# Split projection weights kept in DRAM and read back, and q/k/v products issued in steps of 24 matmuls

## The chip, the cores and the metric

One core of a Trainium2 chip. A core has five engines that run their own instruction streams and wait for each other by semaphores: PE (TensorE, the matrix multiplier), DVE (VectorE), ACT (ScalarE), POOL (GpSimd) and SP (SyncE, which here only issues DMA transfers). Work is held in SBUF (128 partitions) and matmuls add up in PSUM, in banks of 128 x 512 float32. The metric is the device time of one execution in microseconds (us), as the median of several runs.

## The reference

One inference step of a one-layer streaming encoder on 1024 prompt tokens and 64 sample tokens, width 1024, all in float32:

```python
h = _rms_norm(x, norm1_g)
parts = split(h @ w_in)                 # q,k,v (3 x 512), z 512, b 4, a 4, u 256, vm 256, sq 256, sk 128, sv 128
o_a = gated delta rule (q, k, v, a, b)  # 4 heads of 128: state S 128 x 128, blocks of 64 tokens, in sequence
o_b = spatial gating MLP (u, vm)        # 4 heads of 64
o_c = sliding-window attention (sq, sk, sv)
x = x + concatenate([o_a, o_b, o_c]) @ w_out
h = _rms_norm(x, norm2_g)
x = x + (silu(h @ w_gate) * (h @ w_up)) @ w_down      # D_FF 2816
```

The gated delta rule is a recurrence over blocks of 64 tokens: the state S that a block leaves is what the next block starts from, so its steps stand in a chain. The outputs are the new x and the caches and states.

## The kernel before, in words

**Numbers in two parts.** PE multiplies float32 rounded to a shorter format (`fp32r`). To keep float32's accuracy each operand is split into a high part (`h`, a rounded copy) and a low part (`l`, what the rounding left), and a big product is three matmuls: h by xh, h by xl, l by xh.

**Weights.** The class `Weights` holds a list of 84 pieces of [128, up to 1056], in the order of use. `load` issues the raw piece from DRAM by SP (512 KB, line 120) into one of three `wr` buffers; `split` makes the high part on ACT (`hw<-wr`, line 86) and the low part on DVE (`lw<-wr,hw`, line 92), each in two halves of 512 columns, into one of three slots (`hw`/`lw`); `pump`, `run` and `flush` set when a split is put between other work. The in-projection runs over three segments of tokens (384, 384 and 256+64). Each uses the same 24 pieces, in the order: two for the gates and the keys and values of the attention ("g0"), two for its queries ("sq"), twelve for q, k and v of the delta rule ("p"), two "u", two "vm", four "z"; so w_in is loaded and split three times. The out-projection works on w_out in halves of columns: pieces of half 0, of half 1, and once more of half 0 (`wo_plan[0]`, `[1]`, `[2]`, four pieces each, with a fourth slot, `he`/`le`).

**Order of the work.** The whole program is written in the order in which the engines run it. The in-projection's generator (`in_proj`, the main one) and up to a dozen helpers (`aux`) are advanced in turn by `drive`. The helpers are: the convolution of a q, k or v piece (`conv`), the preparation of a block (`prep`), the recurrence (`chain`), attention (`swa`, `q_norm`, `k_norm`) and the gating MLP (`u_evac`, `gmlp`). A round of `drive` is: every helper, in order of its priority, issues its next step as long as the steps of the round need no more than 6 PSUM banks (`ax`); then the main one issues its big matmuls; then each helper of the round goes on to its next halt. So PE's stream alternates between a block of big matmuls (`mm<-xh,hw` and so on) and a set of small ones (mostly `ax<-...`). `fm_group` writes the 24 big matmuls of a piece of q/k/v, u or z in two halves of 12, with a halt in the middle, where a set of small ones is put.

After the in-projection `drain` runs what is left of the helpers. `out_proj` then does 12 jobs of 24 matmuls (128 x 512), and two functions for the last segment's tokens follow: the one on half 1, then the one on half 0 (here "the last piece of the out-projection", which uses `wo_plan[2]`), while ACT and DVE make the operands (`w`, `x`) of the FFN. The FFN uses a scheme of seven products in the manner of Strassen from about 630 us to the end (`x,w` matmuls of line 1462); the change doesn't touch it.

## Time and profile before

| what | value |
|---|---|
| median of 3 runs | 1357.01 us (1356.85 to 1358.77) |
| the profiled execution | 1357.18 us, its span 1355.2 us |
| PE busy | 1316.4 us (97% of the span), 9922 matmuls |
| DVE, ACT, POOL busy | 986.2, 683.4, 183.4 us |
| mean granted clock of TensorE | 0.996 |
| DMA moved | 189.00 MB, of which HBM read 135.72 MB, written 51.61 MB |
| chain that ended last | PE 83%, issue 6%, DVE 5%, ACT 2%, DMA 2% |

How to read it: the in-projection and the recurrence run from the start to about 498 us, the out-projection to about 630 us, the FFN from there on. In rows of groups, `mm<-xh,hw 128*128 128x384` is a matmul into a tile `mm` from the tiles `xh` and `hw`, with the shape of its weights and of its moving operand; `x4` is a count. A row of the timeline has the start, the duration, the engine and line, the instruction, and in brackets the idle time before it and what ended that. Matmuls overlap, so what one adds to PE's time is the distance from its start to the next start, not its duration.

### The profile page before, as it was taken

The page shows a single profiled execution, that of the slowest core. Times are in us where ns is not written, and L with a number is a line of the kernel's source. Part 1 is how long each engine was busy: PE and PEld are TensorE (multiplying, and loading weights), DVE is VectorE, ACT ScalarE, POOL GpSimd, SP SyncE. Part 2 cuts the span into 40 slices and gives each one's busy share as a digit, 9 for nine tenths or more (in the row PEclk, how much of TensorE's full clock was granted, in tenths as well). Part 3 has the DMA queues.
Part 4 walks back from the last instruction along what each step waited for, and adds up shares of the span by engine and source line. Part 5 has one row for each costly group of instructions (what it writes and reads, how often), then busy time and mean ns, then how long its engine had stood idle before and what let it go on. Part 6 is the DMA issues. An engine that isn't in the chain of part 4 may idle for free.

```text
span 1355.2 us, 26537 instructions
## 1 busy us (share of the span) xinstructions
PE 1316.4 (97%) x9922; PEld 1170.9 (86%) x9922; DVE 986.2 (73%) x2286; ACT 683.4 (50%) x1725; POOL 183.4 (14%) x250
## 2 busy tenths in 40 slices
PE   6999999999999999998999999999999988999997
PEld 6988888888878887787999999999999976777784
DVE  6887877867788785588866777667776687767764
ACT  7677376674667653556555554455544532222202
POOL 3100130101121210100000000000000343232104
PEclk9999999999999999998999999999999999999999
DMA  8422342223233161322434544355443499666645
GB/s 259 122 79 64 82 116 78 79 64 80 70 93 94 49 214 51 121 78 86 126 120 152 176 136 124 111 156 175 132 124 112 159 320 335 223 225 238 215 142 198
DMA packets 205011, 189.00 MB, mean 139 GB/s; under 512 B 13931, under 2 KB 174160, under 8 KB 204882
## 3 DMA queue, kind: packets, MB, share of 16 engines
q1 hardware_dynamic: 196690, 174.71, 41.8%
q10 hardware_dynamic: 6704, 8.36, 1.7%
q0 software_dynamic: 1488, 4.23, 0.9%
q8 instruction: 78, 1.28, 0.4%
q14 instruction: 51, 0.42, 0.1%
HBM read 135.72 MB, written 51.61 MB: 138 GB/s over the span
## 4 chain that ended last, share of the span: by engine, by line
PE 83%; issue 6%; DVE 5%; ACT 2%; DMA 2%; POOL 1%; POOLq 0%; SPq 0%; ACTq 0%; DVEq 0%
PE ax L1462 29%; PE mm L95 26%; PE ax L95 11%; PE ax L1775 8%; PE mm L1462 5%; DVE x L92 2%; PE mm L1775 1%; PE ax L503 1%; PE ax L275 1%; DVE lw L92 1%; POOL x L1789 1%; PE ax L838 1%; DMA hd<-w 1%; DMA xs<-in_x_prompt_dram 0%; DVE tr L89 0%
## 5 line engine op out<-in xcount | busy, mean ns | idle before, releaser
L1462 PE MATMUL ax<-x,w 128*128 128x256 f32 (+1 forms) x2552 | 358.6, 287 | 0.0
L1462 PEld LDWEIGHTS ax<-x,w 128*128 128x128 f32 x2552 | 334.2, 190 | 0.3 <-ACT x L86 0.2
L92 DVE TENSOR_TENSOR w<-w,w 128x512 fp32r<-128x512 f32 (+1 forms) x242 | 164.6, 689 | 85.0 <-PE ax L1462 54.1
L95 PE MATMUL mm<-xh,hw 128*128 128x384 f32 (+1 forms) x432 | 151.3, 350 | 0.0
L95 PE MATMUL mm<-xl,hw 128*128 128x384 f32 (+1 forms) x432 | 143.5, 332 | 0.0
L95 PE MATMUL mm<-xh,lw 128*128 128x384 f32 (+1 forms) x432 | 143.1, 331 | 0.0
L92 DVE TENSOR_TENSOR x<-ax,x 128x512 f32<-128x512 f32 (+1 forms) x144 | 98.4, 687 | 58.2 <-PE ax L1775 47.7
L1775 PE MATMUL ax<-x,w 128*128 128x512 f32 x480 | 130.9, 397 | 9.6 <-DVE x L92 9.6
L86 ACT ACTIVATE hw<-wr 128x512 fp32r<-128x512 f32 (+2 forms) x168 | 99.7, 619 | 65.6 <-PE mm L95 55.0
L92 DVE TENSOR_TENSOR lw<-wr,hw 128x512 fp32r<-128x512 f32 (+2 forms) x168 | 110.8, 674 | 25.0 <-ACT hw L86 24.3
L1775 PEld LDWEIGHTS ax<-x,w 128*128 128x128 f32 x480 | 90.3, 190 | 33.1 <-DVE x L92 13.6
L1462 PE MATMUL ax<-xr,w 128*128 128x288 f32 x616 | 116.0, 296 | 1.2 <-DVE s L92 1.2
L86 ACT ACTIVATE w<-w 128x512 fp32r<-128x512 f32 x154 | 94.8, 624 | 31.4 <-PE mm L1462 14.4
L1462 PEld LDWEIGHTS ax<-xr,w 128*128 128x128 f32 x616 | 94.9, 188 | 1.5 <-DVE s L92 1.5
L95 PEld LDWEIGHTS mm<-xh,hw 128*128 128x128 f32 x432 | 81.1, 188 | 10.1 <-issue 7.3
L86 ACT ACTIVATE s<-ax 128x256 f32<-128x256 f32 (+1 forms) x132 | 51.9, 394 | 74.1 <-PE ax L1462 73.7
L95 PEld LDWEIGHTS mm<-xl,hw 128*128 128x128 f32 x432 | 81.4, 189 | 1.3 <-issue 0.7
L95 PEld LDWEIGHTS mm<-xh,lw 128*128 128x128 f32 x432 | 81.1, 188 | 1.2 <-issue 0.3
L1775 PE MATMUL ax<-f,w 128*128 128x512 f32 x220 | 72.5, 399 | 2.8 <-ACT w L86 1.6
L1678 POOL TENSOR_TENSOR w<-x 128x512 f32<-128x512 f32 x6 | 8.9, 1490 | 488.7 <-PE ax L1462 442.1
L1462 PE MATMUL mm<-x,w 128*128 128x256 f32 (+1 forms) x528 | 70.6, 289 | 0.0
L89 DVE SCALAR_TENSOR_TENSOR tr<-tr,cw 128x384 f32<-128x384 f32 (+1 forms) x108 | 64.1, 594 | 7.2 <-ACT tr L86 6.2
(360 smaller groups left out, 2551.0 us busy)
## 6 DMA issues: line engine op xcount, KB each, us to landing
wr<-in_w_in_dram SPq DMA_DIRECT2D x72, 512.0 KB, 3.9
hd<-e SPq DMA_DIRECT2D x140, 256.0 KB, 2.3
w<-hd SPq DMA_DIRECT2D x140, 256.0 KB, 4.6
w<-in_ffn_w_gate_dram SPq DMA_DIRECT2D x44, 256.0 KB, 3.5
w<-in_ffn_w_up_dram SPq DMA_DIRECT2D x44, 256.0 KB, 3.4
x<-in_ffn_w_down_dram SPq DMA_DIRECT2D x12, 512.0 KB, 3.7
wr<-in_w_out_dram SPq DMA_DIRECT2D x9, 512.0 KB, 4.4
y<-in_x_prompt_dram SPq DMA_DIRECT2D x8, 512.0 KB, 7.7
```

The source lines that it names most:

```text
L86: return A.activation(out=out, in_=in_, func=AF.Copy, scale=scale)
L89: return V.scalar_tensor_tensor(out=out, in0=in0, scalar=s, in1=in1, op0=op0, op1=op1)
L92: return V.tensor_tensor(out=out, in0=in0, in1=in1, op=op)
L95: return T.matmul(out, lhsT, rhs, start=start, stop=stop)
L275: T.transpose(b[k // 4][:, (k % 4) * r:(k % 4) * r + r], x[:r, k * 128:k * 128 + 128], ident[:r, :r])
L503: T.transpose(b[u // 4][:, (u % 4) * 128:(u % 4) * 128 + 128], src(u).rearrange("p h i -> p (h i)"), ident)
L838: T.transpose(PTp[0:r0 + cnt, j, kv, :], P[:, kv, 128 * j:128 * j + r0 + cnt], ident)
L1462: T.matmul(ps[:, :NB[c]], a[:, k, :], b[:, k, :], start=first and i == 0, stop=i == 11, skip_group_check=not first)
L1678: eng.tensor_tensor(out=block(t), in0=a, in1=b, op=ALU.subtract)
L1775: T.matmul(ps, l, r, start=fresh and m == 0, stop=m == 3 * len(kps) - 1, skip_group_check=not fresh)
L1789: G.tensor_tensor(out=yf[t][:, c], in0=block(slot), in1=yf[t][:, c], op=ALU.add)
```

## The change

**Kept splits.** A piece that is used again is split once. `keep(i, *later)` gives piece i a DRAM tile `wk` [2, 128, 1056] and notes the later uses in `again`. When piece i is split, SP also writes its high and its low part to that tile (two transfers of 512 KB). A later use issues no raw load and no split: SP reads both parts straight into the slot (two transfers of 512 KB), at the place in the program where the split stood. Kept are: segment 0's p, u, vm and z (20 pieces, read back in segments 1 and 2), segment 1's g0 and sq (4 pieces, read back in segment 2) and `wo_plan[0]` (4 pieces, read back as `wo_plan[2]`). So 36 pieces are split instead of 84, 28 are written, and 48 times a pair is read.

**Whole steps.** For q/k/v of segments 0 and 1 `fm_group` writes all 24 matmuls in one step (`whole`), so a piece has one set of small matmuls behind it and not two.

**Order of the helpers.** `conv` and `u_evac` go first in a round (priority -1) and count no banks; then come those that stand in the middle of a unit of their work (`held`), then the rest. `prep` turns v before the decay factors, and `q_norm` squares in two halves in `tr` buffers.

```diff
+        def keep(self, i, *later):
+            self.kept[i] = tc.dram_tile([2, 128, 1056], F32, name="wk%d" % i)
+            for j in later:
+                self.again[j] = self.kept[i]
         def load(self):
             i = self.nd
+            if i in self.again:
+                self.nd += 1
+                return
...
             h = sb(p, [128, 1056], "h" + t, F32R)
             l = sb(p, [128, 1056], "l" + t, F32R)
-            m = b if i < 2 else n // 2
-            for c in range(0, n, m):
-                acopy(h[:, c:c + m], r[:, c:c + m])
-                tt(l[:, c:c + m], r[:, c:c + m], h[:, c:c + m].bitcast(F32), ALU.subtract)
+            if i in self.again:
+                for j, x in enumerate((h, l)):
+                    SP.dma_start(out=x[:, :n].bitcast(F32), in_=self.again[i][j, :, :n])
+            else:
+                r = self.raw.pop(i)
+                m = b if i < 2 else n // 2
+                for c in range(0, n, m):
+                    acopy(h[:, c:c + m], r[:, c:c + m])
+                    tt(l[:, c:c + m], r[:, c:c + m], h[:, c:c + m].bitcast(F32), ALU.subtract)
+                if i in self.kept:
+                    for j, x in enumerate((h, l)):
+                        SP.dma_start(out=self.kept[i][j, :, :n], in_=x[:, :n].bitcast(F32))
...
+    parts = [pieces(d) for d in plan]
+    for i, j in zip(parts[1][0], parts[2][0]):
+        W.keep(i, j)
+    for i, j, k in zip(*[q[1] for q in parts]):
+        W.keep(i, j, k)
+    for i, j in zip(wo_plan[0], wo_plan[2]):
+        W.keep(i, j)
...
-    def fm_group(xh, xl, n, piece, evac):
+    def fm_group(xh, xl, n, piece, evac, whole=False):
...
-            if kk:
+            if kk and not whole:
                 vstep()
                 W.pump()
                 yield
...
-            if kk == 0:
+            if kk == 0 and not whole:
                 yield
...
-                yield from fm_group(xh, xl, n, piece, lambda ps, a=(s, g, kind, hp): spawn(1, 1, conv(*a, ps)))
+                yield from fm_group(xh, xl, n, piece, lambda ps, a=(s, g, kind, hp): spawn(-1, 0, conv(*a, ps)), s < 2)
...
-            for a in list(aux):
-                if a not in aux:
-                    continue
+            for a in sorted(aux, key=lambda a: 0 if a[0] < 0 else 1 if a in held else 2):
...
                     try:
-                        next(a[2])
+                        if next(a[2]) != "unit":
+                            held.append(a)
```

How the order moves, at the three places of which the prediction speaks.

PE, q/k/v of segment 1. Before, a piece (here `hw_2716`) is cut by a set of small matmuls after 12 big ones. `x4` behind a small matmul counts matmuls in the row:

```order
L95 MATMUL ax<-S_166,KQ 64x128 x4
L95 MATMUL mm<-xh,hw_2716 128x384
L95 MATMUL mm<-xl,hw_2716 128x384
L95 MATMUL mm<-xh,lw_2717 128x384
...
L95 MATMUL mm<-xh,lw_2717 128x384
L95 MATMUL ax<-w,Z 64x128 x2
L95 MATMUL mm<-xh,hw_2716 128x384
L95 MATMUL mm<-xl,hw_2716 128x384
L95 MATMUL mm<-xh,lw_2717 128x384
...
L95 MATMUL mm<-xh,lw_2717 128x384
L95 MATMUL ax<-vn,kt 128x128 x2
```

After, the next set stands 24 big matmuls later, in front of the next piece (`hw_3190`):

```order
L95 MATMUL ax<-S_196,KQ 64x128 x4
L804 MATMUL ax<-cst,qraw 128x128 x6
L95 MATMUL mm<-xh,hw_3125 128x384
L95 MATMUL mm<-xl,hw_3125 128x384
L95 MATMUL mm<-xh,lw_3126 128x384
...
L95 MATMUL mm<-xh,lw_3126 128x384
L95 MATMUL ax<-w,Z 64x128 x2
L95 MATMUL mm<-xh,hw_3190 128x384
```

Counted over PE's whole stream the in-projection had 166 such sets before and has 122 after; the 12 jobs of the out-projection had 18 and have 14. Big and small matmuls are as many as before (2304 and 1645 up to the FFN).

PE, end of the in-projection, from the last big matmul of segment 2 to the first of the out-projection (`hw,oh`). `S,KQ`, `w,Z`, `vn,kt` are links of the recurrence: S gives w, w gives vn, vn gives the next S. Before:

```order
L95 MATMUL mm<-xh,lw_6813 128x320
L95 MATMUL ax<-vn,kt 128x128 x2
L95 MATMUL ax<-vn,at 64x128 x2
L95 MATMUL ax<-Z,tr 32x32 x10
L95 MATMUL ax<-S_165,KQ 64x128 x4
L95 MATMUL ax<-tr 32x32 x10
L95 MATMUL mm<-hw_6910,oh 128x512
```

After, two states (`S_195`, `S_196`) and the sample's (`Ss`) are worked on there, and a link w, a link vn and a link S stand one behind the other with only small matmuls between:

```order
L95 MATMUL mm<-xh,lw_6682 128x320
L95 MATMUL ax<-S_195,KQ 64x128 x4
L95 MATMUL ax<-Z,tr 32x32 x10
L95 MATMUL ax<-wsT,xv 64x64 x4
L95 MATMUL ax<-w,Z 64x128 x2
L95 MATMUL ax<-tr 32x32 x10
L95 MATMUL ax<-vn,kt 128x128 x2
L95 MATMUL ax<-vn,at 64x128 x2
L531 MATMUL ax<-cst,KQ 128x128 x5
L95 MATMUL ax<-Ss_4723,KQ 64x128 x4
L95 MATMUL ax<-S_196,KQ 64x128 x4
L95 MATMUL mm<-hw_6782,oh 128x512
```

Between the last big matmul and `hw,oh` stand ten rows where five stood, and the recurrence's links among them are S, w, vn and S again, where before one vn and one S stood.

DVE, the last piece of the out-projection: the rows from the operands of the first FFN products (`x_8112`, `w_8116` before, `x_8012`, `w_8016` after) to the last sums into `y`. Before:

```order
L92 TENSOR_TENSOR w_8116<-w_8049,w_8115 128x512
L92 TENSOR_TENSOR x_8112<-x_8063,x_8111 128x1024
L92 TENSOR_TENSOR lw_8120<-wr,hw_8119 128x512 x2
L92 TENSOR_TENSOR w_8132<-w_8043,w_8131 128x512
L92 TENSOR_TENSOR w_8136<-w_8071,w_8135 128x512
L92 TENSOR_TENSOR w_8146<-w_8045,w_8145 128x512
L92 TENSOR_TENSOR w_8424<-w_8301,w_8303 128x512
L92 TENSOR_TENSOR y_7077<-mm,y_7077 128x512
L92 TENSOR_TENSOR w_8425<-w_8424,w_8305 128x512
L92 TENSOR_TENSOR w_8301<-w_8305,w_8301 128x512
L92 TENSOR_TENSOR y_7078<-mm,y_7078 128x512
```

After, the low parts `lw` are gone from the stream and both sums into `y` stand ahead of the next `w`:

```order
L92 TENSOR_TENSOR w_8016<-w_7949,w_8015 128x512
L92 TENSOR_TENSOR x_8012<-x_7963,x_8011 128x1024
L92 TENSOR_TENSOR w_8030<-w_7943,w_8029 128x512
L92 TENSOR_TENSOR w_8034<-w_7971,w_8033 128x512
L92 TENSOR_TENSOR w_8044<-w_7945,w_8043 128x512
L92 TENSOR_TENSOR y_7141<-mm,y_7141 128x512
L92 TENSOR_TENSOR y_7142<-mm,y_7142 128x512
L92 TENSOR_TENSOR w_8322<-w_8199,w_8201 128x512
L92 TENSOR_TENSOR w_8323<-w_8322,w_8203 128x512
L92 TENSOR_TENSOR w_8199<-w_8203,w_8199 128x512
```

SP's stream changes with it: in segment 0 two writes (`wk<-hw`, `wk<-lw`, line 153) stand behind every raw load, and the reads of pairs (line 144) stand where a slot comes free.

More of the change, by code (lines that the diff above doesn't have):

```diff
@@ L105, in __init__ @@
             self.retired = None
+            self.kept, self.again = {}, {}
         def slots(self, p, n, tag):
@@ L128, in split @@
             a, b, _ = self.src[i]
-            r, n = self.raw.pop(i), a * b
+            n = a * b
             p, t = self.free.pop(0)
@@ L214, in hybrid_step, with pieces @@
         wo_plan.append(ids)
+    def pieces(d):
+        return d["g0"] + d["sq"], [i for g in range(2) for _, _, i in d["p%d" % g]] + d["u"] + d["vm"] + d["z"]
+    parts = [pieces(d) for d in plan]
[5 more added lines that the diff above has]
+        W.keep(i, j)
     wg_ = w_gate[0].rearrange("(k p) c -> p k c", p=128)
@@ L523, in prep @@
         yield
+        vb = token_major(lambda u: vT[:, u])
+        yield
+        vt = sb(gp, [128, 6, 128], "vt", bufs=2)
+        for u in range(U):
+            acopy(vt[:, u, :], vb[u], scale=irk[:, u:u + 1])
+        yield
         eb = ax()
@@ L529, in prep @@
         A.activation(out=D[:, :N], in_=eb[:, :N], func=AF.Exp)
-        yield
-        vb = token_major(lambda u: vT[:, u])
-        yield
-        vt = sb(gp, [128, 6, 128], "vt", bufs=2)
-        for u in range(U):
-            acopy(vt[:, u, :], vb[u], scale=irk[:, u:u + 1])
         yield
@@ L627, in chain @@
             if s or u:
-                yield
+                yield "unit"
                 b = ax()
@@ L754, in q_norm @@
         nt = qr.shape[1]
-        sq = sb(gp, [128, 12, 64], "vT", bufs=1)
         qf = qr.rearrange("p t (h d) -> p (t h) d", d=64)
-        A.activation(out=sq[:, :4 * nt], in_=qf, func=AF.Square)
         ss = sb(mp, [128, 12], "ssk", bufs=2)
-        V.tensor_reduce(out=ss[:, :4 * nt], in_=sq[:, :4 * nt], axis=AX.X, op=ALU.add)
+        for j in range(2):
+            sq = sb(gp, [128, 390], "tr", bufs=9)
+            sq = sq[:, :128 * nt].rearrange("p (h d) -> p h d", d=64)
+            A.activation(out=sq, in_=qf[:, 2 * nt * j:2 * nt * j + 2 * nt], func=AF.Square)
+            V.tensor_reduce(out=ss[:, 2 * nt * j:2 * nt * j + 2 * nt], in_=sq, axis=AX.X, op=ALU.add)
         gpow(ss[:, :4 * nt], ss[:, :4 * nt], 1.0 / 64, EPS, mhalf)
@@ L806, in swa @@
                     pos += cnt
-            yield
+            yield "unit"
             sc = [ax()[:, off:off + nk] for kv in range(2)]
@@ L1107, in in_seg @@
             yield
-            yield from fm_group(xh, xl, n, P["u"][hb], lambda ps, hb=hb: spawn(2, 0, u_evac(s, hb, ps, n)))
+            yield from fm_group(xh, xl, n, P["u"][hb], lambda ps, hb=hb: spawn(-1, 0, u_evac(s, hb, ps, n)))
             yield
@@ L1134, in drive @@
     def drive(main):
+        held = []
         def advance():
@@ L1159, in drive @@
                 pass
+            del held[:]
             for a in live:
```

## The prediction

> **What bounds the kernel now.** I read the page first, then the busy times by stage, then PE's waits in the longest stage, and last the timeline at the places that the change touches.
>
> ```profile
> PE 1316.4 (97%) x9922; PEld 1170.9 (86%) x9922; DVE 986.2 (73%) x2286; ACT 683.4 (50%) x1725; POOL 183.4 (14%) x250
> ```
>
> PE is busy 97% of the span. The table by stretches (columns: length, busy time and count of PE, its weight loads, DVE, ACT, POOL, then the granted clock, the DMA share and GB/s) tells the stages apart:
>
> ```profile
> 23.00:498.00 475.00, 473.90 (x4505) 410.49 (x4506) 372.38 (x1114) 302.32 (x908) 78.90 (x142) 1.00 0.33 89
> 80.00:120.00 40.00, 40.00 (x430) 34.86 (x428) 32.36 (x83) 25.54 (x77) 0.95 (x5) 1.00 0.30 81
> 480.00:520.00 40.00, 39.98 (x364) 31.48 (x363) 27.62 (x75) 19.65 (x56) 4.52 (x6) 1.00 0.56 194
> 583.00:630.00 47.00, 40.60 (x214) 33.90 (x212) 40.90 (x58) 24.92 (x35) 2.27 (x7) 0.93 0.35 96
> ```
>
> In the in-projection (first row) PE is busy for 473.9 of 475 us at full clock, DMA a third. In the last piece of the out-projection (last row) PE has 6.4 us of idle time and a clock of 0.93. PE's waits in the first stretch (total, times, longest) leave no doubt:
>
> ```profile
> PE ax L95 <- DVE S L89: 0.4, 1, 0.4
> PE ax L95 <- DVE st L92: 0.3, 1, 0.3
> PE mm L95 <- DVE xl L92: 0.2, 1, 0.2
> ```
>
> PE never waits for a split there. That decides the first part.
>
> **The splits of the in-projection: nothing.** There 44 of 72 splits go. What they cost is on two other engines:
>
> ```profile
> L86 ACT ACTIVATE hw<-wr 128x512 fp32r<-128x512 f32 x136 | 82.9, 630 | 46.7 <-PE mm L95 44.8 <-issue 1.9
> L92 DVE TENSOR_TENSOR lw<-wr,hw 128x512 fp32r<-128x512 f32 x134 | 90.5, 686 | 21.2 <-ACT hw L86 20.5
> ```
>
> Two halves each make 88 x 0.63 = 55 us of ACT and 88 x 0.686 = 60 us of DVE. All of it is covered by PE's own work, and PE's waits are 0.9 us together, so I take 0; a gain of those 0.9 us is the most that this relief can bring.
>
> **Fewer sets of small matmuls: -8.9 us.** The matmuls stay as many, but PE changes 48 times less between big and small (44 in the in-projection, 4 in the 12 jobs). What a change costs is read from start to start on PE:
>
> ```profile
> 201.27 0.34 PE L95 MATMUL mm<-xh,lw 128*128 128x384 f32 x1
> 201.53 0.66 PE L95 MATMUL ax<-S,KQ 128*64 128x128 f32 x8
> 202.12 0.44 PE L95 MATMUL mm<-xh,hw 128*128 128x384 f32 x1
> 202.40 0.34 PE L95 MATMUL mm<-xl,hw 128*128 128x384 f32 x1
> 202.58 0.34 PE L95 MATMUL mm<-xh,lw 128*128 128x384 f32 x1
> ...
> 206.83 0.34 PE L95 MATMUL mm<-xh,lw 128*128 128x384 f32 x1
> 207.10 0.49 PE L95 MATMUL ax<-vn,kt 64*128 64x128 f32 x4
> ...
> 208.52 0.42 PE L95 MATMUL mm<-xh,hw 128*128 128x384 f32 x1
> 208.78 0.33 PE L95 MATMUL mm<-xl,hw 128*128 128x384 f32 x1
> ```
>
> Big to big takes 0.18 (202.40 to 202.58; 0.175 on average). Into a set it takes 0.26 and 0.27, on the way back the first big one takes 0.28 and 0.26. So a set costs 0.09 going in and 0.09 to 0.10 coming back, 0.185 us beside its own matmuls, and 48 x 0.185 = 8.9 us. The two sets shown come to 0.19 and 0.18; with a little room for sets of another kind I keep 0.15 to 0.20, that is 7.2 to 9.6 us. That it might be nothing is a rival.
>
> **The last piece of the out-projection: -4.8 us.** Here the splits do stand in the way:
>
> ```profile
> 611.67 0.40 PE L95 MATMUL ax<-hw,oh 128*128 128x512 f32 x1
> 615.42 0.79 PE L95 MATMUL mm<-lw,oh 128*128 128x512 f32 x1 [3.35 <-DVE lw L92]
> 616.01 0.63 PE L95 MATMUL mm<-hw,ol 128*128 128x512 f32 x1
> 616.43 0.63 PE L95 MATMUL mm<-hw,oh 128*128 128x512 f32 x1
> ...
> 621.13 1.72 PE L1462 MATMUL mm<-x,w 128*128 128x256 f32 x12
> ```
>
> PE waits 3.35 us for the low part of the last weights, and goes on at half clock (0.43 us from start to start, where 0.23 was usual: 616.01 to 616.43 against 609.60 to 609.83 below). DVE is late because it works through FFN operands with the splits among them:
>
> ```profile
> 609.60 0.39 PE L95 MATMUL mm<-hw,oh 128*128 128x512 f32 x1
> 609.83 0.39 PE L95 MATMUL mm<-lw,oh 128*128 128x512 f32 x1
> ```
>
> ```profile
> L92 DVE TENSOR_TENSOR lw<-wr,hw 128x512 fp32r<-128x512 f32 x8 | 5.2, 686 | 0.0
> ```
>
> ```profile
> 614.67 1.29 DVE L92 TENSOR_TENSOR lw<-wr,hw 128x512 fp32r<-128x512 f32 x2
> 615.88 2.49 DVE L92 TENSOR_TENSOR w<-w,w 128x512 fp32r<-128x512 f32 x4
> 618.29 0.69 DVE L92 TENSOR_TENSOR y<-mm,y 128x512 f32<-128x512 f32 x1
> ```
>
> All eight go. A pair holds DVE for 615.88 - 614.67 = 1.21 us, so DVE is 4 x 1.21 = 4.8 us ahead at the sum into `y` (618.29), on which the norm, the transposes and the FFN's flow hang. PE alone would allow more: without the wait and at 0.23 us the 14 steps from 611.67 end at 614.9, where 621.13 stood, 6.2 us. DVE is the tighter one, so -4.8; bounds 0 (the stall only changes its cause) and -6.2. The reads that take the place of the raw loads start when a slot comes free. The last of them gets the slot of this stage's first piece, and two pieces of 16 steps lie between that piece's end and the use: 2 x 16 x 0.23 = 7.4 us, in which two transfers have to land. The nearest row lands in 3.9 us:
>
> ```profile
> wr<-in_w_in_dram SPq DMA_DIRECT2D x72, 512.0 KB, 3.9
> ```
>
> SP also holds one FFN gate load behind the second of these reads, and so it can be a piece (16 x 0.23 = 3.7 us) later. DVE has other operands to make in that time, so I price it at nothing; without that cover up to 3.7 us of the gain would go, which is inside the bounds.
>
> **What is paid: +1.0, +2.0, +1.5 us.** First, the links of the recurrence left at the end of the in-projection. One link takes, from PE's start to DVE's or ACT's result:
>
> ```profile
> 202.24 0.35 DVE L89 SCALAR_TENSOR_TENSOR w<-ax,ne,vt 128x128 f32<-128x128 f32 x1 [0.32 <-PE ax L95]
> 204.43 0.44 PE L95 MATMUL ax<-w,Z 64*64 64x128 f32 x4
> 204.91 0.37 ACT L86 ACTIVATE vn<-ax,b 128x128 f32<-128x128 f32 x1 [1.15 <-PE ax L95]
> 207.64 0.71 DVE L89 SCALAR_TENSOR_TENSOR S<-S,eg,ax 128x128 f32<-128x128 f32 x2 [0.48 <-PE ax L95]
> ```
>
> S to w 202.59 - 201.53 = 1.06, w to vn 205.28 - 204.43 = 0.85, vn to S 208.35 - 207.10 = 1.25, together 3.2 us. Among big matmuls they are covered; now only small sets of about 0.4 to 0.6 us each lie between, which leaves 0.3 to 0.4 of each link open: +1.0, bounds 0 and 3.2.
>
> Second, the second query piece of segment 2. Its pair is read into the slot of the first gate piece, which PE gives back late: 8 gate matmuls, a set and 12 query matmuls ahead of the use. At 0.12 us (two rows below) and 0.9 for the set that is 20 x 0.12 + 0.9 = 3.3 us, while the two reads take 4 to 6 (3.9 for one transfer, 2 more for the second behind it). Before, the raw load had been there long ago. I take +2.0, bounds 0 and 4.3.
>
> ```profile
> 352.15 0.28 PE L95 MATMUL mm<-lw,xh 128*128 128x264 f32 x1
> 352.27 0.28 PE L95 MATMUL mm<-hw,xh 128*128 128x264 f32 x1
> ```
>
> Third, the DMA queues in segment 0. A piece now loads 0.52 MB and writes 1.05 MB. The second row of the table by stretches moves 81 GB/s at a share of 0.30, so 270 GB/s when full (raw loads, mostly); the third 194 at 0.56, so 346 (rows of 4 KB, as the written ones). That makes 0.52/270 + 1.05/346 = 1.94 + 3.03 = 4.97 us a piece. PE's pace there, by its big matmuls:
>
> ```profile
> 35.70:119.80 84.10, 65.54 (x336) 57.83 (x336) 0.00 (x0) 6.48 (x14) 1.00 0.36 95
> ```
>
> 336 matmuls are 14 pieces in 84.1 us, 6.0 each; at the least, 24 x 0.175 with a small set behind, some 4.45. So the queue keeps up on average, and behind short steps it runs 0.5 us late. If PE paid that at all twelve q/k/v pieces it would be 6 us; the three raw buffers take up most of it: +1.5, bounds 0 and 6. The Trainium skill (DMA: Bandwidth & Descriptors, "Where 436 GB/s comes from") gives about 358 GB/s as what memory allows a core for such transfers; by that figure a piece would be an estimated 1.57 MB / 358 = 4.4 us and this term 0, so the sum 1.5 lower. No row here is that fast for raw loads.
>
> **Sum**, against the profiled execution (1357.18 us, of which the span is 1355.2; the median is 1357.01, so the same): 1357.2 - 8.9 - 4.8 + 1.0 + 2.0 + 1.5 = **1348.0 us**. With the bounds put together so that not all fall on one side, its own range is 1341 to 1354.
>
> **Rivals.**
>
> *The stall at the out-projection stays.* The reads wait for a slot that PE gives back, where raw loads waited only for a buffer; if the pair lands later than PE needs it, or DVE waits for the sums of PE instead, nothing is won there: 1348.0 + 4.8 = 1352.8. For it speaks the DVE order, in which sums into `y` stand among the operands; against it 7.4 us of lead. The Trainium skill (TensorE: Matmul & The Clock Gate, Part 1) says an idle window of about 3.4 us halves the clock; the row with 3.35 us idle and 0.43 us steps after it agrees, so such a wait would cost about twice its length.
>
> *Fewer sets save nothing.* The recurrence needs its links in order, and a set holds one link of each state; with fewer sets more links come back at the end or as waits for DVE inside larger sets. Then 8.9 us are lost again: 1356.9. Against it speaks the count of sets over the whole stream, which takes in the end.
>
> *Slower: the writes set the pace of segment 0.* It decides from 6.0 us of transfers a piece. One transfer alone lands in 3.9 us (raw) and the nearest for a write is this:
>
> ```profile
> yd<-y SPq DMA_DIRECT2D x8, 512.0 KB, 2.6
> ```
>
> If nothing overlapped a piece took 3.9 + 2 x 2.6 = 9.1 us; half way between that and 4.97 it is 7.0, one more than PE's 6.0, and with 20 pieces 20 us: 1348.0 - 1.5 + 20 = 1366.5. For it: raw load and writes go through one queue, and SP issues the writes ahead of the next raw load. Against it: in the FFN one stretch moves 334 GB/s at a share of 0.96 with writes and reads mixed, by which a piece takes 4.7:
>
> ```profile
> 1090.00:1150.00 60.00, 49.99 (x221) 40.14 (x221) 47.93 (x74) 15.60 (x33) 17.64 (x14) 0.97 0.96 334
> ```
>
> **Chances and range.** Forecast 0.56, stall stays 0.16, sets save nothing 0.10, slower 0.11, something better or another wait 0.07. A measurement of this kernel tells 0.2% (2.7 us) from no change, so faster means below 1354.3. Faster: forecast nearly whole (0.54), first rival mostly (0.13), others 0.06, together 0.73. Same: 0.14, mostly the second rival. Slower: 0.13, the third with half of what is unnamed. The range takes in the first two rivals and leaves the third out: 1340 to 1357.
>
> **What would show it.** Right: fewer sets (about 48 changes less) and an earlier end of the in-projection by 5 to 9 us; no PE wait for `lw` near 611 us and a full clock there; the DMA share of segment 0 near 0.8 with no wait of PE for it; one wait of PE for a read pair in segment 2 of about 2 us. Wrong: PE waits behind `hw<-wk` or `lw<-wk` reads in many places, waits for DVE `S` or `w` inside small sets, or raw loads of segment 0 landing well over 6 us after their issue.

## The result, and the profile after

The changed kernel takes 1350.59 us (median of 5 runs, 1349.55 to 1352.15) where the kernel before took 1357.43 (5 runs beside it): the ratio is 0.995, with a 95% interval of 0.9935 to 0.9964. Measured again beside other runs (e9 below) it was 0.9951 (0.9937 to 0.9965). That is 6.8 us faster. The prediction said 1348.0, range 1340 to 1357.

The page of the changed kernel, first the engines, then the transfers (KB each, median us from issue to landing):

```profile
PE 1312.1 (97%) x9922; PEld 1175.0 (87%) x9922; DVE 931.3 (69%) x2193; ACT 636.5 (47%) x1632; POOL 175.3 (13%) x250
...
lw<-wk SPq DMA_DIRECT2D x46, 512.0 KB, 4.5
hw<-wk SPq DMA_DIRECT2D x46, 512.0 KB, 3.6
wr<-in_w_in_dram SPq DMA_DIRECT2D x28, 512.0 KB, 7.1
wk<-hw SPq DMA_DIRECT2D x25, 512.0 KB, 5.8
```

DVE lost 54.9 us of work and ACT 46.9, and PE 4.3; PE is still the engine that is busy throughout. The stages show where it moved. The rows are segment 0, segment 1, segment 2 and the 12 jobs of the out-projection, cut at PE's first gate matmul of each segment, its first `hw,oh` and its first transpose of the sums. Before:

```profile
14.20:168.80 154.60, 153.33 (x1437) 137.00 (x1437) 122.34 (x341) 100.47 (x282) 21.10 (x38) 1.00 0.40 108
168.80:341.80 173.00, 172.98 (x1628) 148.78 (x1626) 133.72 (x389) 109.22 (x322) 25.63 (x43) 1.00 0.30 82
341.80:497.60 155.80, 155.01 (x1505) 131.51 (x1503) 124.28 (x401) 97.67 (x313) 34.27 (x65) 1.00 0.31 87
497.60:582.90 85.30, 85.30 (x450) 63.89 (x449) 45.85 (x104) 43.83 (x97) 9.72 (x18) 1.00 0.36 128
```

After:

```profile
14.10:162.90 148.80, 148.42 (x1381) 136.04 (x1381) 114.93 (x315) 97.93 (x273) 20.61 (x36) 1.00 0.81 270
162.90:329.00 166.10, 165.96 (x1576) 147.17 (x1575) 102.85 (x321) 82.36 (x264) 20.81 (x41) 1.00 0.50 171
329.00:495.00 166.00, 164.38 (x1633) 138.51 (x1631) 115.46 (x419) 85.02 (x303) 27.96 (x64) 1.00 0.47 163
495.00:578.70 83.70, 83.47 (x430) 63.21 (x428) 42.92 (x96) 42.91 (x89) 12.45 (x24) 1.00 0.34 125
```

Segments 0 and 1 are 5.8 and 6.9 us shorter, and segment 2 is 10.2 us longer: PE runs 56 and 52 matmuls fewer in the first two and 128 more in the third. Whole steps let the recurrence fall behind, and its links are made up for in segment 2: the two kernels below that leave whole steps out have 1491 (e1) and 1505 matmuls (e4) there, where the kernel before had 1505. By the first transpose the gain is 582.9 - 578.7 = 4.2 us. The marks on PE (us from the span's start; e-numbers are the experiments) go on from there:

| PE starts | before | after | e1 | e3 | e4 | e5 | e7 | e10 |
|---|---|---|---|---|---|---|---|---|
| segment 1 | 168.8 | 162.9 | 170.3 | 163.4 | 168.8 | 161.9 | 163.3 | 163.0 |
| segment 2 | 341.8 | 329.0 | 342.7 | 330.4 | 341.0 | 327.7 | 330.4 | 329.9 |
| out-projection | 497.6 | 495.0 | 497.1 | 502.7 | 494.6 | 503.3 | 501.1 | 507.2 |
| transposes of the sums | 582.9 | 578.7 | 583.9 | 586.4 | 579.9 | 583.6 | 584.7 | 590.9 |
| FFN's flow (25th `x,w`) | 629.9 | 620.9 | 626.1 | 628.7 | 622.1 | 625.8 | 632.0 | 633.1 |
| last matmul | 1350.3 | 1343.0 | 1347.7 | 1350.8 | 1345.1 | 1350.5 | 1354.7 | 1356.9 |

From the transposes to the FFN's flow it is 47.0 us before and 42.2 after: 4.8 us, the out-projection's stall. The FFN then takes 720.4 us before and 722.1 after. From the 25th to the 3001st product it is 450.2 or 450.3 us in every profile but those of e11 and e12, where the count starts elsewhere; the rest of the FFN takes 270.1 to 274.4 us over all fourteen profiles, 270.1 before, 271.8 and 270.8 in the two of the changed kernel (with a granted clock of 0.99, 0.98 and 0.99 in its last 270 us). So 9.0 us are won by the FFN's flow and 7.3 are left at the end; of the 1.7 us between, 1.0 is a difference that two runs of one kernel show as well.

PE's waits in the changed kernel up to 640 us (total, times, longest; the two at the program's start left out):

```profile
PE ax L303 <- ACT wr L86: 4.5, 3, 2.4
PE ax L95 <- DVE w L89: 0.8, 2, 0.6
PE ax L95 <- DVE PT L873: 0.5, 1, 0.5
PE ax L95 <- DVE tr L590: 0.4, 1, 0.4
PE mm L95 <- DVE xl L92: 0.2, 1, 0.2
PE ax L868 <- ACT P L86: 0.2, 1, 0.2
```

No row has a read pair or a raw load: PE waits for no transfer. The wait for `lw` is gone, and at its place PE flows at 0.23 us and then waits for ACT's scaled sums:

```profile
610.10 0.39 PE L95 MATMUL ax<-hw,oh 128*128 128x512 f32 x1
610.33 0.40 PE L95 MATMUL ax<-lw,oh 128*128 128x512 f32 x1
610.57 1.64 PE L1494 MATMUL mm<-x,w 128*128 128x256 f32 x12
614.55 1.09 PE L303 MATMUL ax<-cst,wr 128*128 128x128 f32 x8 [2.35 <-ACT wr L86]
616.08 1.09 PE L303 MATMUL ax<-cst,wr 128*128 128x128 f32 x8 [0.43 <-ACT wr L86]
...
620.27 0.71 PE L303 MATMUL ax<-cst,wr 64*128 64x64 f32 x8 [1.67 <-ACT wr L86]
```

**PE's time by kinds of step.** The distance from each matmul to the next start can be put in classes, by whether it and the next are big (`mm`) or small; a big one's is parted into the usual distance of its shape and what goes beyond that. Summed over all of PE's rows from segment 0 to the first transpose, us (and how many):

| class | before | after | e1 | e4 | e5 | e7 | e10 |
|---|---|---|---|---|---|---|---|
| big, at the usual distance of its shape | 357.7 | 357.7 | 357.7 | 357.7 | 357.5 | 357.6 | 357.9 |
| beyond that, into a set | 18.1 (184) | 12.8 (136) | 18.7 (160) | 17.5 (166) | 14.3 (134) | 15.4 (140) | 15.1 (138) |
| beyond that, first big one behind a set | 16.9 | 12.7 | 14.9 | 15.9 | 13.4 | 13.2 | 13.8 |
| small to small, same tiles | 120.5 | 123.2 | 121.9 | 121.0 | 123.4 | 122.5 | 124.3 |
| small to small, other tiles | 28.7 (175) | 37.0 (219) | 32.0 (196) | 29.0 (184) | 39.0 (210) | 38.3 (222) | 41.2 (226) |
| last small to big | 25.2 (183) | 18.8 (135) | 22.8 (159) | 22.7 (165) | 19.3 (134) | 19.6 (140) | 19.6 (137) |
| rest, big to big | 1.4 | 1.9 | 1.3 | 1.5 | 1.9 | 3.6 | 4.8 |
| between the marks | 568.7 | 564.6 | 569.6 | 565.7 | 569.4 | 570.5 | 576.7 |

PE's waits are inside these classes, and the classes of a column add up to 0 to 0.6 us less than its last row. From before to after, 48 sets fewer take 5.3 + 4.2 = 9.5 us off the ends of the sets, 0.198 each; the prediction had 0.185. But 44 more steps go from one group of small matmuls to another (+8.3), and only 48 fewer from the last small one to a big one (-6.4). A step to other small tiles takes 0.164 to 0.169 us, one within a group 0.05, one to a big matmul 0.138. A joined set thus keeps its inner boundary. With the longer steps inside groups (+2.7, waits among them) and the rest, 5.1 of the 9.5 us are given back; between the marks 4.1 us are left. In e4 it went otherwise: with 18 sets fewer only 9 steps to other tiles came, the ends take 1.6 and the last steps to a big one 2.5 us less, and 3.0 us are left between the marks, 0.17 a set, though by other terms than the prediction's.

### The profile page after: what moved, and what is told of

It is laid out like the page before. It is cut to its first block, busy times and chain, and to the rows that moved or that the text cites. A ratio compares the mean times of both kernels' runs of the same rounds, so it can differ in the third digit from the quotient of the medians.

```text
span 1348.0 us, 26507 instructions
## 1 busy us (share of the span) xinstructions
PE 1312.1 (97%) x9922; PEld 1175.0 (87%) x9922; DVE 931.3 (69%) x2193; ACT 636.5 (47%) x1632; POOL 175.3 (13%) x250
## 4 chain that ended last, share of the span: by engine, by line
PE 83%; DVE 6%; issue 6%; POOL 2%; ACT 2%; DMA 1%; POOLq 0%; DVEq 0%; ACTq 0%
PE ax L1494 29%; PE mm L95 26%; PE ax L95 11%; PE ax L1807 9%; PE mm L1494 5%; DVE x L92 2%; PE mm L1807 2%; PE ax L303 1%; PE ax L531 1%; POOL x L1821 1%; DVE w L92 1%; PE ax L868 1%; DVE tr L89 1%; DMA xs<-in_x_prompt_dram 0%; DMA hd<-w 0%
## 5 line engine op out<-in xcount | busy, mean ns | idle before, releaser
L1494 PEld LDWEIGHTS mm<-x,w 128*128 128x128 f32 x528 | 67.9, 190 | 0.2 <-issue 0.2
L95 PE MATMUL mm<-hw,xh 128*128 128x256 f32 (+1 forms) x216 | 62.9, 296 | 0.0
```

The source lines that it names most:

```text
L95: return T.matmul(out, lhsT, rhs, start=start, stop=stop)
L1494: T.matmul(ps[:, :NB[c]], a[:, k, :], b[:, k, :], start=first and i == 0, stop=i == 11, skip_group_check=not first)
```

## The experiments

The theory after this profile: the out-projection's 4.8 us are DVE's low parts; the sets give about half of what was thought; the rest is not known, since whole steps, the new order of the helpers and the relief of ACT and DVE came together. Each was taken away or put in alone.

**e1, halves.** Whole steps off.

```diff
-                yield from fm_group(xh, xl, n, piece, lambda ps, a=(s, g, kind, hp): spawn(-1, 0, conv(*a, ps)), s < 2)
+                yield from fm_group(xh, xl, n, piece, lambda ps, a=(s, g, kind, hp): spawn(-1, 0, conv(*a, ps)))
```

> The changed kernel with q/k/v in two halves of 12 matmuls again in every segment; kept splits and the new order of the helpers stay. Its order has 24 sets of small matmuls more than the changed kernel (168 against 144). Theory of the prediction: 0.185 us a set, +4.4 us on 1350.6, so 1355.0. Rival 1: a set saves 0.19 us at its ends but gives back about 0.06 us, because the joined set has one boundary more between groups of small matmuls: 24 x 0.127 = +3.0, so 1353.6. Rival 2: sets cost nothing, 1350.6.

Measured: 1355.81 us, ratio to before 0.9985 (0.9975 to 0.9995), so 4.7 us slower than the changed kernel by the ratios. The time is near the first theory's, yet not for its reason: the ends of sets (18.7 + 14.9 against 12.8 + 12.7) cost 8.1 us more, though 24 sets at 0.198 are 4.8, and 3.3 of it are waits and other steps. PE's waits show them:

```profile
PE ax L868 <- ACT P L86: 1.7, 3, 1.0
PE ax L95 <- DVE tr L590: 1.3, 2, 0.7
PE ax L95 <- DVE w L89: 1.2, 2, 0.9
```

They sum to 4.2 here, and the same three to 1.4 in the changed kernel.

**e2, w_out split twice.** The pieces of w_out are not kept.

```diff
-    for i, j in zip(wo_plan[0], wo_plan[2]):
-        W.keep(i, j)
```

> The changed kernel, but the pieces of w_out's first half are loaded raw and split a second time in the last piece of the out-projection, as before. Theory: +4.8 us (8 low parts on DVE in front of the sums), 1355.4, with PE waiting for lw again near 610 us. Rival: the stall there was not DVE's, 1350.6.

Measured: 1356.04 us, 0.9981 (0.9972 to 0.999), 4.2 us by the ratios. On PE the stall is back, with the half clock behind it:

```profile
611.04 0.79 PE L95 MATMUL mm<-lw,oh 128*128 128x512 f32 x1 [3.32 <-DVE lw L92]
611.63 0.63 PE L95 MATMUL mm<-hw,ol 128*128 128x512 f32 x1
612.06 0.63 PE L95 MATMUL mm<-hw,oh 128*128 128x512 f32 x1
...
625.72 6.50 PE L1492 MATMUL ax<-x,w 128*128 128x256 f32 x51
```

Its FFN's flow starts at 625.7 with the transposes at 578.6, 47.1 us apart as before (47.0). The four kept pieces are worth 4.9 us there.

**e3, only w_out kept.** The in-projection splits every piece in every segment again; whole steps and the new order stay.

```diff
-    for i, j in zip(parts[1][0], parts[2][0]):
-        W.keep(i, j)
-    for i, j, k in zip(*[q[1] for q in parts]):
-        W.keep(i, j, k)
```

> The changed kernel, but every piece of the in-projection is loaded raw and split in every segment; only w_out's four pieces are kept, and whole steps and the new order stay. Its order has 5 sets more (149 against 144). Theory: 44 splits on ACT and DVE are covered by PE, so +0.9 us for the sets, 1351.5; if the reads and writes of pairs cost what the prediction charged (3.5 us), 1348.0. Rival: the relief of ACT and DVE shortens the links of the recurrence, 1354 or more.

Measured: 1356.64 us, 0.999 (0.9981 to 0.9999): 5.4 us slower than the changed kernel by the ratios, as the rival had it. By the marks segment 1 is 0.9 and segment 2 is 6.3 us longer. What hangs on ACT's work there is seen at e10.

**e4, kept splits alone.** The kernel before with `keep`, `again` and the list of kept pieces, as the diff ahead of the prediction has them; steps of 12, and the helpers as before. On the kernel before:

```diff
+    parts = [pieces(d) for d in plan]
+    for i, j in zip(parts[1][0], parts[2][0]):
+        W.keep(i, j)
+    for i, j, k in zip(*[q[1] for q in parts]):
+        W.keep(i, j, k)
+    for i, j in zip(wo_plan[0], wo_plan[2]):
+        W.keep(i, j)
```

> The kernel before with kept splits alone: two halves of 12 and the old order of the helpers. Its order has 174 sets where before had 193 and the changed kernel has 144. Theory: -4.8 us in the out-projection and 19 sets x 0.185 = -3.5, so 1357.4 - 8.3 = 1349.1 without any charge for DMA, 1352.6 with the 3.5 us charged. Rival (sets save nothing): 1352.6 without the charge.

Measured: 1351.09 us, 0.9948 (0.9936 to 0.9961). The kept splits alone give the whole gain. By the marks 3.0 us come by the transposes and 4.8 from there to the FFN's flow. Its PE order has 174 sets up to the FFN where before had 193 (the table, which ends at the first transpose, has 166 and 184), though its generators are written as before: the order on an engine isn't only the written one, as the description ahead of the prediction has it; with reads in place of loads and splits the build put the instructions otherwise. Why it came out with fewer sets is not known.

**e5, whole steps with the old order.** The priorities and banks of `conv` and `u_evac` and the round of `drive` are those of before; the edits in `prep` and `q_norm` stay.

```diff
-                yield from fm_group(xh, xl, n, piece, lambda ps, a=(s, g, kind, hp): spawn(-1, 0, conv(*a, ps)), s < 2)
+                yield from fm_group(xh, xl, n, piece, lambda ps, a=(s, g, kind, hp): spawn(1, 1, conv(*a, ps)), s < 2)
...
-            yield from fm_group(xh, xl, n, P["u"][hb], lambda ps, hb=hb: spawn(-1, 0, u_evac(s, hb, ps, n)))
+            yield from fm_group(xh, xl, n, P["u"][hb], lambda ps, hb=hb: spawn(2, 0, u_evac(s, hb, ps, n)))
...
-            for a in sorted(aux, key=lambda a: 0 if a[0] < 0 else 1 if a in held else 2):
+            for a in list(aux):
+                if a not in aux:
+                    continue
```

> The changed kernel with the old order of the helpers (conv and u_evac with their old priorities and a bank, no helper first because it stands in the middle of a unit); kept splits and whole steps stay. Its order has 143 sets (e4: 174, e1: 168, changed kernel 144). Theory now: the new order costs 4.7 us (e1 against e4) and a set is worth 0.085 us net, so e4 less 31 x 0.085 = 2.6 us: 1348.5, with before at 1358.4. Rival: the new order is what lets whole steps pay, since it serves the recurrence first; without it links come late and PE waits: 1353 or more.

Measured: 1356.11 us, 0.9984 (0.9974 to 0.9993). The theory fell, the rival is right. Segment 2 (third row by stages) is the place:

```profile
327.70:503.30 175.60, 170.35 (x1692) 143.77 (x1690) 117.40 (x416) 92.31 (x340) 30.01 (x67) 0.99 0.51 175
```

It is 9.6 us longer than in the changed kernel; PE is idle for 5.2 us of it (1.6 in the changed kernel), and 59 more matmuls are left for it. PE's two longest waits for helpers from 14 to 640 us, of which the first and 0.8 us of the second stand in segment 2:

```profile
PE ax L95 <- DVE xv L92: 2.7, 1, 2.7
PE ax L95 <- DVE tr L590: 1.4, 3, 0.8
```

So whole steps (e5) cost 5 us on top of e4, the new order (e1) costs 5 us on top of e4, and both together cost nothing. (`prep` and `q_norm` are as changed in e1 and e5 and as before in e4, so a part of either 5 us may be theirs; that was not tried.) Beside the kept splits the pair wins nothing that these runs can tell.

**e6, writes doubled.** Each kept piece is written a second time to a place that nobody reads.

```diff
-            self.kept[i] = tc.dram_tile([2, 128, 1056], F32, name="wk%d" % i)
+            self.kept[i] = tc.dram_tile([4, 128, 1056], F32, name="wk%d" % i)
...
-                    for j, x in enumerate((h, l)):
+                    for j, x in enumerate((h, l, h, l)):
                         SP.dma_start(out=self.kept[i][j, :, :n], in_=x[:, :n].bitcast(F32))
```

> The changed kernel, but each kept piece is written twice (a second copy that nobody reads), 2.1 MB instead of 1.05. By the rates of the prediction's third rival a piece of segment 0 then takes 1.94 + 6.06 = 8.0 us of transfers against 6 of PE, so 20 x 2 = +40 us, near 1390. Rival: the queue has far more room than these rates say, under +5 us, 1356 at most.

Measured: 1385.85 us, 1.0208 (1.0191 to 1.0225), 35 us slower than the changed kernel. Segment 0 is 27.8 us longer, its DMA share 0.93, and now PE waits for the splits there, which are late:

```profile
14.10:190.70 176.60, 158.48 (x1381) 140.59 (x1381) 113.40 (x311) 97.15 (x269) 19.52 (x36) 0.97 0.93 326
```

```profile
PE mm L95 <- ACT hw L86: 8.2, 5, 1.7
PE mm L95 <- DVE lw L92: 6.6, 6, 1.4
```

PE's 6.4 us a piece in segment 0 of the changed kernel ((162.9 - 35.6) / 20) plus 27.8 / 20 is 7.8, near the 8.0 us that the two rates of the prediction give. But that is an average, and not a proof of the rates: from 35 to 100 us, where the DMA engines are busy throughout (the share counts a packet whole where it starts, so it can exceed 1), they move 388 GB/s, by which 2.62 MB take 6.8 us:

```profile
35.00:100.00 65.00, 55.01 (x329) 50.25 (x329) 42.31 (x106) 36.81 (x104) 6.90 (x13) 0.97 1.05 388
```

Behind 100 us the share is 0.85, and the granted clock of 0.97 over all of segment 0 can stand for up to 5 of the 27.8 us. What set the pace there stays open. The cliff of the third rival is real; the changed kernel stands in front of it at a share of 0.81.

**e7, whole steps and new order alone.** Nothing is kept (e2 and e3 together).

```diff
-    for i, j in zip(parts[1][0], parts[2][0]):
-        W.keep(i, j)
-    for i, j, k in zip(*[q[1] for q in parts]):
-        W.keep(i, j, k)
-    for i, j in zip(wo_plan[0], wo_plan[2]):
-        W.keep(i, j)
```

> Whole steps and the new order alone: every piece loaded raw and split at each use. Its order has 150 sets (before 193). Theory now: without the relief of ACT and DVE segment 2 loses its time to waits and extra sets as in e3 (3.5 us more than before by the start of the transposes), and the stall of the out-projection is back: 1358.4 + 3.5 = 1361.9, slower than before. Theory of the prediction (44 splits are covered, a set is worth 0.185): 1358.4 - 8.0 = 1350.4.

Measured: 1361.10 us, 1.0025 (1.0016 to 1.0034): slower than before, as expected from e3, though not at the places expected: by the marks it loses 1.8 us by the transposes where 3.5 were expected, and the rest behind them. Without the kept splits the other two thirds of the change lose 3 us. Segment 2 again:

```profile
330.40:501.10 170.70, 166.91 (x1633) 138.56 (x1631) 138.64 (x463) 105.33 (x345) 32.17 (x64) 1.00 0.30 85
```

DVE is busy 138.64 of 170.70 us there, 81%, where in the changed kernel it is 115.46 of 166.00, 70%.

**e8, whole steps in half of segment 2 as well**, on e5.

```diff
-                yield from fm_group(xh, xl, n, piece, lambda ps, a=(s, g, kind, hp): spawn(1, 1, conv(*a, ps)), s < 2)
+                yield from fm_group(xh, xl, n, piece, lambda ps, a=(s, g, kind, hp): spawn(1, 1, conv(*a, ps)), s < 2 or g == 0)
```

> e5 with whole steps in the first half of segment 2's q/k/v too: 126 sets, 17 fewer than e5. Theory: 17 x 0.085 = 1.4 us faster than e5, 1347.1. Rival: fewer sets in segment 2 leave more links of the recurrence for the end, where nothing covers them: 2 us or more slower than e5.

Measured: 1360.79 us, 1.0022 (1.0012 to 1.0031), 5 us slower than e5 though its order has 17 sets fewer. Segment 2 takes 190.3 us where e5's takes 175.6 (the jobs of the out-projection, 6.2 us shorter, win a part back); PE is idle for 9.6 us of it, and the granted clock there is 0.97. Fewer sets are no gain where the recurrence's links are what is left.

**e9, the changed kernel again**, with no edit, measured beside the next three.

> The changed kernel once more, beside the three others of this call. All theories: 0.995 of before (1350.6 against 1357.4), within 1 us.

Measured: 1351.17 us, 0.9951 (0.9937 to 0.9965).

**e10, the load of the splits without the splits.** For each piece of the in-projection that is read back, ACT and DVE do the work of a split into a buffer that nobody reads (one of the three `wr`, in turn with the raw loads).

```diff
+                if i < wo_plan[0][0]:
+                    scr = sb(wp, [128, 1056], "wr", bufs=3)
+                    for c in range(0, n, n // 2):
+                        acopy(scr[:, c:c + n // 2], h[:, c:c + n // 2].bitcast(F32))
+                        tt(scr[:, c:c + n // 2], scr[:, c:c + n // 2], l[:, c:c + n // 2].bitcast(F32), ALU.subtract)
```

> The changed kernel, but for each of the 44 pieces of the in-projection that are read back, ACT copies and DVE subtracts in two halves of 512 columns into a buffer that nobody reads: the load of the splits on ACT and DVE is back, their data, loads and slots are not. Theory now: it is the load on ACT and DVE that segment 2 of e3 paid for, so 5 to 6 us slower than the changed kernel, near e3's 0.999 of before. Rival: the raw loads and the wait for a split's own result cost it, then no slower than 1 us. Theory of the prediction (covered): no slower than 1 us.

Measured: 1360.15 us, 1.0021 (1.0008 to 1.0034), 9 us slower than e9. Segment 2:

```profile
329.90:507.20 177.30, 170.84 (x1633) 141.90 (x1632) 139.77 (x463) 107.31 (x347) 31.11 (x64) 0.97 0.47 160
```

PE's longest waits for helpers from 14 to 640 us, all but 0.3 us of them in segment 2:

```profile
PE ax L95 <- DVE w L89: 3.1, 3, 2.2
PE mm L95 <- ACT tr L86: 1.6, 1, 1.6
PE ax L873 <- ACT P L86: 1.4, 1, 1.4
```

No weight hangs on this work, and PE waits for none: it waits for `w`, `tr` and `P`, links of the helpers that stand behind it on DVE and ACT. So neither the raw loads nor PE's wait for a split's result is needed for the loss. But the work is not all that e10 puts back: its copy on ACT waits until the pair's high part has landed, and all that stands behind it on ACT waits with it. The first row is from segment 2 of e10 (total, times, longest), the second is the copy ahead of the 2.2 us wait for `w`, and the third is from segment 2 of e3, where ACT stands still too, until PE gives back a slot:

```profile
ACT wr L86 <- DMA hw<-wk: 16.8, 12, 3.5
390.69 1.15 ACT L86 ACTIVATE wr<-hw 128x512 f32<-128x512 f32 x2 [3.47 <-DMA hw<-wk]
ACT hw L86 <- PE mm L95: 18.2, 13, 3.2
```

So putting the splits on ACT and DVE is enough for the loss, by their work or by what they hold up while they wait; these runs do not part the two. That e10 loses more than e3 (9 against 5 us) shows in two numbers: PE's waits in segment 2 are 6.2 us against 3.4, and from 395.3 to 405.5 us, around the 2.2 us wait, the granted clock is 0.50, where e3 has 0.99 over its segment 2.

**e11 and e12, the FFN's first products ahead of the last transposes.** An attempt to fill the 4.5 us that PE waits for ACT at 614 to 620 us, on the changed kernel and on e4: the three products are issued together and the transposes of the last three token tiles behind them.

```diff
-        b = x_transpose(yn, r)
+        while t >= 6 and "begun" not in flags:
+            yield
+        if t >= 6:
+            with tc.issue_after(marks["begun"].ins):
+                b = x_transpose(yn, r)
+        else:
+            b = x_transpose(yn, r)
...
-            yield
             begun[k]()
-            yield
+        flags.add("begun")
+        yield
+        yield
```

> The changed kernel with the three first products of the FFN (36 matmuls) all ahead of the transposes of the last three token tiles on PE, where before one stood ahead and two between. In the changed kernel PE waits 4.5 us for ACT there (three waits) and the FFN's flow starts 10.3 us after its first product. Theory: two products of 12 matmuls (1.7 us each) fill the waits: 3.3 us faster than the changed kernel, 1347.3. Rival: the chain from the sums to the transposes ends the stage anyway, and the products behind it are no sooner: 0 to 1 us.

> e4 (kept splits alone) with the same products ahead of the transposes. In e4 PE waits 3.0 us for ACT there. Theory: 2 to 3.3 us faster than e4's 0.9948 of before: 0.9925. Rival: 0 to 1 us.

Measured: e11 1350.91 us, 0.9956 (0.9943 to 0.997), no different from e9; e12 1351.45, 0.9959 (0.9946 to 0.9971), none from e4. The first two waits are filled and the third grows:

```profile
615.02 1.04 PE L303 MATMUL ax<-cst,wr 128*128 128x128 f32 x8
616.23 1.09 PE L303 MATMUL ax<-cst,wr 128*128 128x128 f32 x8 [0.18 <-ACT wr L86]
619.95 0.70 PE L303 MATMUL ax<-cst,wr 64*128 64x64 f32 x8 [2.63 <-ACT wr L86]
```

The last tile's transposes stand at 619.95 where they stood at 620.27 (620.10 in e9): the chain from its sums over ACT and POOL ends the stage. What the products moved ahead had saved PE lost behind it: it waited 0.5 us for ACT's operands of the second block of tokens, and its stretch of lower clock came later. The 18 us from 622 us on in e11:

```profile
622.00:640.00 18.00, 17.48 (x125) 17.10 (x125) 17.35 (x19) 13.93 (x22) 0.00 (x0) 0.92 0.03 3
```

and in e9, the changed kernel (141 matmuls where e11 ran 125):

```profile
622.00:640.00 18.00, 18.00 (x141) 17.72 (x140) 17.66 (x19) 14.72 (x25) 0.00 (x0) 1.00 0.06 17
```

In the 14 us before it is the other way round, 0.99 in e11 and 0.88 in e9; but there PE had waits for ACT in any case, and behind 622 us it has none in e9.

No kernel tried beats the changed one beyond its interval; e4, a third of the change, equals it.

## Why the prediction was right or wrong, point by point

**The out-projection, -4.8 us: right.** 47.0 to 42.2 us by the marks, and e2 puts 4.9 back. DVE was the bound and its four pairs of low parts the price, at 1.21 us a pair. e2 puts ACT's high parts back as well, but in the kernel before DVE is busy for 36.84 of the 37.30 us up to the end of its last sum into `y`, ACT for 18.41:

```profile
583.50:620.80 37.30, 33.95 (x160) 27.85 (x159) 36.84 (x51) 18.41 (x26) 0.47 (x2) 0.92 0.36 96
```

The first of the two last sums into `y` starts 35.4 us behind the first transpose before and 31.0 after. PE's 6.2 us were not to be had, since the chain over `y`, ACT and POOL ends the stage (e11 shows the same from the other side).

**The sets, -8.9 us: the price was gross.** The step that failed is the one from "a set costs 0.185 us beside its own matmuls" to 48 times that. The ends do cost that (9.5 us measured for 48), but what a set holds isn't the same when two are joined: the last small matmul of the first set, which went to a big one in 0.137 us, now goes to other small tiles in 0.165 or more, so of the two steps at the seam only the excess at the ends is saved. That and the steps inside the groups took 5.1 us back, of which 1.2 are waits (1.9 us of PE's waits for helpers after, 0.7 before). The bounds 7.2 to 9.6 were taken from two sets' ends alone, and no row of a boundary between small groups was put against them. In e4, where fewer boundaries came in their place, a set came to 0.17 us, more by the last steps than by the ends. And the second rival, sets save nothing, was nearer the truth than its chance: as a part of the whole, joined sets with the new order gave nothing (e4 against the changed kernel).

**The splits of the in-projection, 0: wrong for the changed kernel.** The step that failed is the inference from PE's waits before to a kernel with another order: 0.9 us of waits in the kernel before said that there was no more to win, and in e4, with steps and helpers as before, waits gave nothing: PE's waits up to the out-projection are 2.8 us there and 1.9 before, and the 3.0 us that e4 wins by the transposes are fewer sets. That the reads would change PE's order so, the prediction did not see. But the change itself moved the recurrence into segment 2 and made its links dense there. With the splits that stage loses 4.7 us (e7: 170.7 against 166.0) to 6.3 us (e3), and e10 shows that it needs no wait of PE for a split: what stands behind the splits on ACT and DVE comes late. Cover that was there before the change wasn't there after it. I named what hid the work, and not what the work would cost when the cover moved.

**The end of the in-projection, +1.0: right in kind.** At the place itself one wait stands (0.56 us), inside the bounds 0 and 3.2; the others stand earlier in segment 2, where the prediction had none, 1.2 us more in all.

```profile
490.62 0.45 PE L95 MATMUL ax<-wsT,xv 64*64 64x64 f32 x8
491.63 0.44 PE L95 MATMUL ax<-w,Z 64*64 64x128 f32 x4 [0.56 <-DVE w L89]
```

**The second query piece of segment 2, +2.0: not paid.** SP issues the pair when the slot comes free, as worked out, and PE takes its first matmul 4 us later. But then it runs small sets before it needs the low part:

```profile
340.76 0.32 SPq L144 DMA_DIRECT2D hw<-wk  x1
341.17 0.38 SPq L144 DMA_DIRECT2D lw<-wk  x1
```

```profile
344.76 0.39 PE L95 MATMUL mm<-hw,xh 128*128 128x256 f32 x1
345.07 0.48 PE L95 MATMUL ax<-vn,kt 64*128 64x128 f32 x2
...
346.69 0.41 PE L95 MATMUL mm<-lw,xh 128*128 128x256 f32 x2
```

The order of the changed kernel had those small matmuls between the two (`vn,kt`, `vn,at`, `w,Z`, `P`), and the prediction counted only what stood ahead of the first.

**The queues of segment 0, +1.5: not paid.** The DMA share was foretold at near 0.8 and is 0.81; raw loads land in 7.1 us instead of 3.9, and three buffers take that up without a wait of PE. e6 shows what there was to fear; the two rates, 270 and 346 GB/s, were too low, since 388 were moved there. The Trainium skill's figure (DMA: Bandwidth & Descriptors, "Where 436 GB/s comes from", about 358 GB/s a core) would have put a piece of e6 at an estimated 2.62 MB / 358 = 7.3 us; it took 7.8 by the marks, but the 388 GB/s of the busiest stretch are above that figure too.

**The sum.** By the transposes the prediction had -8.9 + 1.0 + 2.0 + 1.5 = -4.4 and the trace has -4.2. That they agree is luck, two errors against each other: 3.9 us of the sets' gain were given back beyond the waits, and 3.5 us of transfers were charged that nobody paid. The FFN's flow came 9.0 us earlier, the sum said 9.2. The rest of the miss, 1348.0 against 1350.6, is the last 270 us of the FFN, where the profiled execution lost 1.7 us, and the spread of the runs. The time fell inside the range, then, with one term out of three by its mechanism (the out-projection), one at twice its size (the sets) and one cause that the prediction put at nothing (the splits).

**The signs.** No wait for `lw`, a full clock at the out-projection and a DMA share near 0.8 came as named. The in-projection's end came 2.6 us earlier (497.6 to 495.0), not 5 to 9, and no wait for a read pair came. Raw loads that land well over 6 us after their issue were named as a sign of being wrong; they came (7.1 us), and cost PE no wait.

## What to carry to other kernels

An engine that covers work before a change may not cover it after: price the hidden work again with the order that the change makes, and with what it holds up behind it while it waits, above all where a chain is packed into fewer, denser places. The price of an interruption has to be taken net: what does the interrupting work itself cost when it is put behind other work of its kind? And take a change of several parts apart: here one part alone gave all of the gain, and the two others, each harmful alone beside it, cancelled.

## What the runs showed of the hardware that was not expected

From one small matmul's start to the next took 0.05 us with the same tiles, 0.165 us when the next reads other tiles, and 0.137 us when the next is a big one (sums over some 2400, 200 and 150 steps of the changed kernel and the kernel before). The waits of PE are in these means. So a change of small operands costs at least as much as leaving the set.

A wait of 2.63 us in e11 was followed by a granted clock of 0.92 over the next 18 us. The prediction had the half clock behind a wait of 3.35 us and named the Trainium skill's idle window of about 3.4 us (TensorE: Matmul & The Clock Gate, Part 1); here a shorter single wait was followed by it too, and what else fell into the window the runs don't show. In the two profiles of the changed kernel the same wait at the same place, 2.35 us in one and 2.36 in the other, was followed once by full clock (1.00 from 608 to 622 us) and once not (0.88 in the same stretch). So a wait's length alone did not decide it.
